# The opening rows of a fused matmul and layer norm: the last quarter of A turned by the DMA, sums put aside twice, late casts on another engine

## The chip, the cores and the metric

The kernel runs on one core of a Trainium2 chip. The metric is the time of one execution on the device in microseconds (us), the median of several runs. A profile is one further execution, recorded by the hardware: it lists every instruction of every engine with its start and its length, what it waited for, and every packet of the sixteen DMA engines.

The engines, as the profile names them: PE (the matrix unit; PEld is its loading of weights), DVE (vector), ACT (scalar), POOL (general) and SP, which here does nothing but issue DMA transfers. Each engine works through its own instructions strictly in the order of the program. Engines wait for each other and for transfers through semaphores.

## The reference

```python
x = np.matmul(a, b)                       # a, b: 2048 x 2048, float32
mean = np.mean(x, axis=-1, keepdims=True)
var = np.var(x, axis=-1, keepdims=True)
normalized = (x - mean) / np.sqrt(var + eps)
return (gamma * normalized + beta).astype(np.float32)
```

A row of the result needs the whole row of the product before its mean and variance are known.

## The kernel before

**Tiling.** A is cut into 16 row blocks of 128 rows ("rows" below, index i or p), the inner dimension into 16 k tiles of 128 (kt), the columns of B into 4 quarters of 512 (q, 0 to 3). One matmul takes one k tile of one row (128 x 128, turned so that k lies on the partitions) and one k tile of one quarter of B (128 x 512), and adds into one PSUM bank. There are 16 x 16 x 4 = 1024 of them, and eight banks. Operands are float16, sums float32. B as float16 (`b16`) stays in SBUF for the whole kernel.

**Two phases.** The first five rows (R = 5, the opening) are worked on together while B comes in: every k tile of B that lands is used by five rows. From row 5 on, all of B is there, and a row is done quarter by quarter, 16 matmuls each.

**The opening, before.** Quarter 3 is called MAIN, quarters 0, 1 and 2 ASIDE. The order of PE's work, written out by hand, is: quarters 0, 1, 2 for k tiles 0 to 3, each row's sum copied to SBUF by ScalarE (`put_aside`, L261 in the profile); then MAIN for all 16 k tiles, each row's sum copied out by `evacuate` (L95) with its statistics by VectorE (L96); then quarters 0, 1 and 2 for k tiles 4 to 15, where VectorE adds the bank to what was put aside (L265) and takes statistics (L266) in `add_rest`. After quarter 2 each row also gets its mean and variance (`stats`), and its normalisation is queued as two pieces in `backlog`, which later rows drain.

**How A gets turned.** For the opening, A comes in four chunks of four k tiles, in float32; VectorE casts a chunk to float16 (L186, L194), PE turns it with four transposes for each row (`turn`, L243), and ScalarE copies the result from PSUM to `at` (L245). From row 5 on, POOL issues a DMA that loads a whole row and casts it on the way (`a16`, L345), and SP issues a DMA transpose from `a16` to `at` (`turn_ahead`, L412). POOL's loads are held back by `gate`, a one-column copy (L255) that waits until the last block of B has landed.

**How B comes in.** `load_b2` moves two k tiles of one quarter (512 KB) into one of six staging buffers (tile `stb`, issued by SP, L203) and VectorE casts it to `b16` (L205). A staging buffer is free for the next load when its cast is done. SP also waits, at each issue, for the transfer that it issued eight before to have landed: DMA semaphores go round in eights. The blocks that come after MAIN's are in a list, `later`; `bring(n)` issues the next n of them, at fixed spots between the rows of PE's order, so that the casts lie in VectorE's order between the `add_rest` work of rows.

**After the last block of B** SP issues `gamma_b` and `beta_b` (1 MB each), four small rows of the same vectors, and then the DMA transposes of rows 5 and 6, which need POOL's loads.

Of the kernel before, what the change touches and what calls it, by code (L numbers as in the profile page):

```python
# [11 lines left out]
AluOp = mybir.AluOpType  # L12
# [4 lines left out]
def kernel(  # L17
# [9 lines left out]
    nc = tc.nc  # L27
# [5 lines left out]
    n_kt = K // P  # L33
    NB = 512
    n_nb = N // NB
    NH = N // 2
    KC = 4
    KW = KC * P
    n_kc = n_kt // KC
    R = 5  # L40
    ASIDE, MAIN = (0, 1, 2), 3
# [21 lines left out]
    gate = konst.tile([P, 1], FP32)  # L63
    gamma_b = konst.tile([P, N], FP32)
    beta_b = konst.tile([P, N], FP32)
    b16 = bpool.tile([P, n_kt, N], FP16)

    pair = {}
    xs = [None] * n_mt
    bnst = [None] * n_mt  # L70
    acc = {}

    def bank(name):
        return psum.tile([P, NB], FP32, tag="ps", name=name)
# [4 lines left out]
    def at(i):  # L79
        return pair[i // 2][:, i % 2]  # L80

    def mm(i, q, kt, first, last):
        if (i, q) not in acc:
            acc[i, q] = bank(f"acc{i}_{q}")
        nc.tensor.matmul(  # L85
            acc[i, q], at(i)[:, kt, :], b16[:, kt, ds(q * NB, NB)],
            start=first, stop=last,
        )

    def evacuate(i, q):  # L90
        if xs[i] is None:
            xs[i] = xpool.tile([P, N], FP32, tag="x", name=f"x{i}")
            bnst[i] = stat.tile([P, n_nb, 6], FP32, tag="bnst", name=f"bnst{i}")
        qs = ds(q * NB, NB)
        nc.scalar.copy(xs[i][:, qs], acc[i, q])  # L95
        nc.vector.bn_stats(bnst[i][:, q, :], xs[i][:, qs])  # L96
# [3 lines left out]
    def stats(i):  # L100
        mv = stat.tile([P, 2], FP32, tag="mv", name=f"mv{i}")
        nc.vector.bn_aggr(mv, bnst[i])  # L102
        ve = stat.tile([P, 1], FP32, tag="ve", name=f"ve{i}")
        nc.vector.tensor_tensor(ve, mv[:, 1:2], eps_t, AluOp.add)  # L104
        sq = stat.tile([P, 1], FP32, tag="sq", name=f"sq{i}")
        nc.scalar.activation(sq, ve, ActFn.Sqrt)  # L106
        return mv, sq

    def centre(i, q, mv):
        qs = ds(q * NB, NB)  # L110
        nc.vector.scalar_tensor_tensor(  # L111
            xs[i][:, qs], xs[i][:, qs], mv[:, 0:1], gamma_b[:, qs],
            AluOp.subtract, AluOp.mult)

    def scale(i, q, rstd):
        qs = ds(q * NB, NB)
        nc.vector.scalar_tensor_tensor(  # L117
            xs[i][:, qs], xs[i][:, qs], rstd, beta_b[:, qs],
            AluOp.mult, AluOp.add)

    def store(i, q0, nq):
        s = ds(q0 * NB, nq * NB)
        nc.sync.dma_start(out[ts(i, P), s], xs[i][:, s])

    def inv(i, sq):
        rstd = stat.tile([P, 1], FP32, tag="rstd", name=f"rstd{i}")
        nc.vector.reciprocal(rstd, sq)
        return rstd

    def queue_norm(i, mv, sq):  # L130

        got = {}

        def piece(q0):
            def run():
                centre(i, q0, mv)
                centre(i, q0 + 1, mv)
                if q0 == 0:
                    got["rstd"] = inv(i, sq)
                scale(i, q0, got["rstd"])  # L140
                scale(i, q0 + 1, got["rstd"])
                store(i, q0, 2)
            return run

        backlog.extend(piece(q) for q in range(0, n_nb, 2))
# [20 lines left out]
    a16_of = {}  # L166
# [15 lines left out]
    def load_a1(i, c):  # L182
        st = half_stage()
        nc.sync.dma_start(st, a[ts(i, P), ts(c, KW)])  # L184
        a16_room(i, c)
        nc.vector.tensor_copy(a16_of[i, c], st)  # L186

    def load_a2(i, c):
        st = stg.tile([P, 2, NB], FP32, tag="st", name=f"sta{i}_{c}")
        nc.sync.dma_start(  # L190
            st, a[ds(i * P, 2 * P), ts(c, KW)].rearrange("(t p) k -> p t k", p=P))
        for m in (0, 1):
            a16_room(i + m, c)
        nc.vector.tensor_copy(held["a"][:, ds(i % KC, 2), :], st)  # L194
# [3 lines left out]
        nc.sync.dma_start(st, b[ts(k, P), 0:NB])  # L198
        nc.vector.tensor_copy(b16[:, k, 0:NB], st)  # L199

    def load_b2(k, q):
        st = stg.tile([P, 2, NB], FP32, tag="st", name=f"stb{q}_{k}")
        nc.sync.dma_start(  # L203
            st, b[ds(k * P, 2 * P), ds(q * NB, NB)].rearrange("(t p) n -> p t n", p=P))
        nc.vector.tensor_copy(b16[:, k:k + 2, ds(q * NB, NB)], st)  # L205
        return st

    pairs = [list(range(i, min(i + 2, R))) for i in range(0, R, 2)]

    def load_pair(j, c):  # L210
        if len(pairs[j]) == 2:
            load_a2(pairs[j][0], c)
        else:
            load_a1(pairs[j][0], c)
# [4 lines left out]
        load_b2(0, q)  # L219
        load_b2(2, q)  # L220
    load_pair(0, 1)
    for c in range(n_kc):
        load_b2(c * KC, MAIN)
        if c + 1 < n_kc:
            load_pair(0 if c > 0 else 1, c + 1)
        load_b2(c * KC + 2, MAIN)
        if c + 1 < n_kc:
            if c > 0:
                load_pair(1, c + 1)
            load_pair(2, c + 1)  # L230

    warm = bank("warm")

# [4 lines left out]
    def turn(rows, c):  # L238
        n = len(rows)
        t_ps = psum.tile([P, n, KC, P], FP16, tag="ps", name=f"tps{rows[0]}_{c}")  # L240
        for m, i in enumerate(rows):
            for j in range(KC):
                nc.tensor.transpose(t_ps[:, m, j, :], a16_of[i, c][:, ts(j, P)], ident)  # L243
        i0 = rows[0]
        nc.scalar.copy(  # L245
            pair[i0 // 2][:, ds(i0 % 2, n), ds(c * KC, KC), :], t_ps)

    later = [(k, q) for q in ASIDE for k in range(0 if q == MAIN else KC, n_kt, 2)]

    def bring(n):  # L250
        for _ in range(n):
            k, q = later.pop(0)
            st = load_b2(k, q)
            if not later:
                nc.gpsimd.tensor_copy(gate, st[:, 0, 0:1])  # L255

    def put_aside(p, q):
        if xs[p] is None:
            xs[p] = xpool.tile([P, N], FP32, tag="x", name=f"x{p}")
            bnst[p] = stat.tile([P, n_nb, 6], FP32, tag="bnst", name=f"bnst{p}")  # L260
        nc.scalar.copy(xs[p][:, ds(q * NB, NB)], acc.pop((p, q)))  # L261

    def add_rest(p, q):
        qs = ds(q * NB, NB)
        nc.vector.tensor_tensor(xs[p][:, qs], acc[p, q], xs[p][:, qs], AluOp.add)  # L265
        nc.vector.bn_stats(bnst[p][:, q, :], xs[p][:, qs])  # L266
# [23 lines left out]
    for q in ASIDE[1:]:  # L290
# [3 lines left out]
        for p in range(R):  # L294
            for kt in range(2, KC):
                mm(p, q, kt, False, kt == KC - 1)
            put_aside(p, q)


    spots = {(0, 4): 0, (1, 1): 1, (1, 4): 2}  # L300
    for h in (0, 1):
# [3 lines left out]
            if (h, p) in spots:  # L305
                turn(pairs[spots[h, p]], 1)
    spots = {(1, 4): 0, (2, 4): 1, (3, 1): 2}
    for kt in range(KC, n_kt - KC):
        for p in range(R):
            mm(p, MAIN, kt, False, False)  # L310
            if (kt % KC, p) in spots:
                turn(pairs[spots[kt % KC, p]], kt // KC + 1)
    for kt in range(n_kt - KC, n_kt - 2):
        for p in range(R):
            mm(p, MAIN, kt, False, False)
    for p, n in enumerate((1, 1, 0, 1, 0)):
        for kt in (n_kt - 2, n_kt - 1):
            mm(p, MAIN, kt, False, kt == n_kt - 1)
        bring(n)
        evacuate(p, MAIN)  # L320


    for q, k_row, ahead, asked in (
            (0, n_kt - KC, 7, (0, 0, 1, 0, 1)), (1, 2 * KC, 2, (0, 1, 1, 1, 1))):
        bring(ahead)
        for kt in range(KC, k_row):
            for p in range(R):
                mm(p, q, kt, kt == KC, False)
        for p in range(R):
            for kt in range(k_row, n_kt):  # L330
                mm(p, q, kt, False, kt == n_kt - 1)
            bring(asked[p])
            add_rest(p, q)
    assert not later
    nc.sync.dma_start(gamma_b, gamma.unsqueeze(0).to_broadcast([P, N]))
    nc.sync.dma_start(beta_b, beta.unsqueeze(0).to_broadcast([P, N]))
    if eps_ap is not None:
# [61 lines left out]
    def quarter(i, q):  # L399
        for kt in range(n_kt):  # L400
            mm(i, q, kt, kt == 0, kt == n_kt - 1)
# [6 lines left out]
    def turn_ahead(t):  # L408
        if R <= t < n_mt:
            if t % 2 == 0:  # L410
                new_pair(t // 2)
            nc.sync.dma_start_transpose(at(t), a16[t])  # L412

    turn_ahead(R)
    turn_ahead(R + 1)
    for p in range(R):
        for kt in range(KC, n_kt):
            mm(p, ASIDE[2], kt, kt == KC, kt == n_kt - 1)
        add_rest(p, ASIDE[2])
        queue_norm(p, *stats(p))  # L420
    for i in range(R, n_mt):
        last = i == n_mt - 1
        turn_ahead(i + 2)
        for q in range(n_nb):
            quarter(i, q)
            if last and q == n_nb - 1:
                break
            evacuate(i, q)
            if q < n_nb - 1:
                drain(1)  # L430
            if last:
                scaled(i, q)
        if last:
            drain(len(backlog))
            finish_row(i)
        else:
            close(i)
# [35 lines left out]
```

## Time and profile before

| what | value |
|---|---|
| time, median of 3 runs | 246.57 us (246.26 to 246.64) |
| the profiled execution's own time | 246.04 us |
| span of its instructions | 244.0 us |
| PE busy | 236.1 us, 97% of the span |
| DVE busy | 175.3 us, 72% |
| ACT busy | 52.0 us, 21% |
| granted PE clock, mean over the span | 0.994 |
| moved by DMA | 52.64 MB, 216 GB/s on the mean |

The span is the time from the first to the last recorded instruction; the 2.0 us between it and the execution's time lie around it. The page also cuts the span into 40 slices of 6.1 us: PE is busy in tenths of 9 in all but the first and the last, and DMA in tenths of 9 in slices 2 to 17, that is up to about 100 us, with the rate near 385 GB/s up to about 50 us and falling behind it. A group line names the source line, the engine, the operation and the tiles, then busy time, mean length of one, and the idle time of the engine just before these instructions with what ended it. A timeline line gives start and length in us, and in brackets the idle time before it and who ended that.

### The profile page before, as it was taken

Reading aid. Unit: us, or ns where it says so; the run is one execution under the profiler, and the core shown is the slowest. Engines: PE = TensorE matmul, PEld = TensorE weight load, DVE = VectorE, ACT = ScalarE, POOL = GpSimd, SP = SyncE. Lnnn points to the kernel's source line nnn. Section 1 sums busy time; section 2 is a strip of 40 time slices with the busy share of each in tenths; the row PEclk is TensorE's granted clock in tenths of the full one; section 3 lists DMA queues with packets and bytes.
Section 4 is the critical chain, followed back from the end, with each engine's and each line's share of the span. In section 5 each row is a group of like instructions: output and inputs, shape, how many; then the busy total and the mean of one; then the engine's idle time right before and its main releaser. Section 6 shows DMA issues by size and latency. Waiting matters only on the chain.

```text
span 244.0 us, 2967 instructions
## 1 busy us (share of the span) xinstructions
PE 236.1 (97%) x1133; PEld 107.7 (44%) x1133; DVE 175.3 (72%) x310; ACT 52.0 (21%) x96; POOL 7.0 (3%) x17
## 2 busy tenths in 40 slices
PE   7899999999999999999999999999999999999982
PEld 2344555444444444444444444444444444444430
DVE  1544554969997589999999995937557391947873
ACT  2466445400000011212120211112111211112100
POOL 0000000000300100000000000000000000000000
PEclk9999999999999999999999999999999999999997
DMA  5999999999999999898989898683907144220405
GB/s 118 395 387 387 387 381 385 379 309 364 375 261 179 159 131 262 245 230 216 232 220 272 134 291 174 202 194 64 257 4 197 60 128 132 82 90 0 176 0 172
DMA packets 41190, 52.64 MB, mean 216 GB/s; under 512 B 24404, under 2 KB 24404, under 8 KB 40920
## 3 DMA queue, kind: packets, MB, share of 16 engines
q1 hardware_dynamic: 39592, 46.68, 60.1%
q0 software_dynamic: 1584, 5.77, 15.2%
q8 instruction: 9, 0.15, 0.3%
q14 instruction: 5, 0.04, 0.1%
HBM read 35.67 MB, written 16.78 MB: 215 GB/s over the span
## 4 chain that ended last, share of the span: by engine, by line
PE 94%; DMA 2%; DVE 1%; SPq 0%; issue 0%; ACT 0%
PE acc L85 91%; DMA st<-in_a_dram 2%; PE tps L243 2%; PE w L385 1%; DVE x L395 0%; DVE bnst L369 0%; DVE x L372 0%; DVE a16s L186 0%; PE warm L236 0%; SPq L198 0%; SPq L184 0%; PE nm_ps L380 0%; DVE mv L102 0%; ACT lead L381 0%; DVE nm L377 0%
## 5 line engine op out<-in xcount | busy, mean ns | idle before, releaser
L85 PE MATMUL acc<-b,at 128*128 128x512 f16 x1024 | 223.2, 379 | 0.9 <-DVE b L199 0.9
L85 PEld LDWEIGHTS <-at 128*128 128x128 f16 x1024 | 99.6, 98 | 119.3 <-ACT at L245 1.4
L96 DVE BATCH_NORM_STATS2 bnst<-x 128x6 f32<-128x512 f32 x48 | 32.9, 689 | 33.4 <-ACT x L95 33.3
L95 ACT COPY x<-acc 128x512 f32<-128x512 f32 x48 | 27.8, 588 | 108.8 <-PE acc L85 107.5
L117 DVE SCALAR_TENSOR_TENSOR x<-x,rstd,beta_b 128x512 f32<-128x512 f32 x61 | 43.1, 747 | 0.5
L111 DVE SCALAR_TENSOR_TENSOR x<-x,mv,gamma_b 128x512 f32<-128x512 f32 x60 | 42.0, 742 | 0.0
L205 DVE CAST b<-stb 128x1024 f16<-128x1024 f32 x30 | 20.4, 688 | 11.2 <-DMA stb<-in_b_dram 11.1
L106 ACT ACTIVATE sq<-ve 128x1 f32<-128x1 f32 x16 | 3.2, 203 | 55.3 <-DVE ve L104 55.3
L245 ACT COPY at<-tps 128x512 f16<-128x512 f16 (+1 forms) x14 | 10.6, 770 | 14.1 <-PE tps L243 13.8
L265 DVE TENSOR_TENSOR x<-acc,x 128x512 f32<-128x512 f32 x15 | 10.3, 686 | 3.0 <-PE acc L85 2.9
L266 DVE BATCH_NORM_STATS2 bnst<-x 128x6 f32<-128x512 f32 x15 | 10.4, 694 | 0.5
L345 POOL DMA_DIRECT2D a<-in_a_dram x11 | 6.3, 576 | 91.7 <-DMA at<-a 91.3
L236 PE MATMUL warm<-zeros 128*128 128x512 f16 x23 | 7.7, 478 | 1.2 <-DVE zeros L152 1.2
L261 ACT COPY x<-acc 128x512 f32<-128x512 f32 x15 | 7.6, 607 | 5.1 <-PE acc L85 5.1
L186 DVE CAST a16s<-st 128x512 f16<-128x512 f32 x8 | 3.4, 427 | 6.1 <-DMA st<-in_a_dram 5.9
L243 PEld LDWEIGHTS <-a16s 128*128 128x128 f16 x80 | 5.2, 98 | 4.4 <-DVE a16s L186 2.3
L194 DVE CAST a16s<-sta 128x1024 f16<-128x1024 f32 x6 | 4.2, 695 | 4.1 <-DMA sta<-in_a_dram 4.1
L243 PE MATMUL tps<-ident,a16s 128*128 128x128 f16 x80 | 6.8, 220 | 0.2
L236 PEld LDWEIGHTS <-zeros 128*128 128x128 f16 x23 | 2.5, 115 | 4.9 <-issue 2.7
L102 DVE BATCH_NORM_AGGREGATE mv<-bnst 128x2 f32<-128x24 f32 x16 | 4.2, 264 | 0.5
L199 DVE CAST b<-st 128x512 f16<-128x512 f32 x4 | 1.7, 427 | 2.3 <-DMA st<-in_b_dram 2.3
L104 DVE TENSOR_TENSOR ve<-mv,eps_t 128x1 f32<-128x1 f32 x16 | 2.5, 159 | 0.5
(26 smaller groups left out, 16.8 us busy)
## 6 DMA issues: line engine op xcount, KB each, us to landing
stb<-in_b_dram SPq DMA_DIRECT2D x30, 512.0 KB, 6.5
out_dram<-x SPq DMA_DIRECT2D x30, 512.0 KB, 3.0
a<-in_a_dram POOLq DMA_DIRECT2D x11, 512.0 KB, 7.2
sta<-in_a_dram SPq DMA_DIRECT2D x6, 512.0 KB, 6.4
st<-in_a_dram SPq DMA_DIRECT2D x8, 256.0 KB, 7.2
st<-in_b_dram SPq DMA_DIRECT2D x4, 256.0 KB, 6.3
gamma_b<-in_gamma_dram SPq DMA_DIRECT2D x1, 1024.0 KB, 6.8
beta_b<-in_beta_dram SPq DMA_DIRECT2D x1, 1024.0 KB, 10.3
```

The costliest lines, as they stand in the source:

```text
L85: nc.tensor.matmul(acc[i, q], at(i)[:, kt, :], b16[:, kt, ds(q * NB, NB)], start=first, stop=last,)
L95: nc.scalar.copy(xs[i][:, qs], acc[i, q])
L96: nc.vector.bn_stats(bnst[i][:, q, :], xs[i][:, qs])
L111: nc.vector.scalar_tensor_tensor(xs[i][:, qs], xs[i][:, qs], mv[:, 0:1], gamma_b[:, qs], AluOp.subtract, AluOp.mult)
L117: nc.vector.scalar_tensor_tensor(xs[i][:, qs], xs[i][:, qs], rstd, beta_b[:, qs], AluOp.mult, AluOp.add)
L205: nc.vector.tensor_copy(b16[:, k:k + 2, ds(q * NB, NB)], st)
L236: nc.tensor.matmul(warm if to is None else to, zeros[:, 0:P], zeros, start=True, stop=True)
L243: nc.tensor.transpose(t_ps[:, m, j, :], a16_of[i, c][:, ts(j, P)], ident)
L245: nc.scalar.copy(pair[i0 // 2][:, ds(i0 % 2, n), ds(c * KC, KC), :], t_ps)
L261: nc.scalar.copy(xs[p][:, ds(q * NB, NB)], acc.pop((p, q)))
L265: nc.vector.tensor_tensor(xs[p][:, qs], acc[p, q], xs[p][:, qs], AluOp.add)
L266: nc.vector.bn_stats(bnst[p][:, q, :], xs[p][:, qs])
```

## The change

The opening is put in another order, and three pieces of work go to other places.

- Chunk 3 of A (k tiles 12 to 15 of the five rows) is still loaded and cast as before, but PE no longer turns it. SP issues one DMA transpose of 128 x 512 for each row instead (`turn_last`, five in all), between the issues of late blocks of B.
- MAIN stops after k tile 11 and is put aside; quarter 0 continues with k tiles 4 to 11 and is added to what was put aside (`add_part`, the same vector addition as L265 without statistics). Quarters 1 and 2 run from 4 to 15 as before, with the last four k tiles row by row. Then MAIN and quarter 0 get k tiles 12 to 15, row by row, with `add_rest`; the last one also closes the row (`close_opening`).
- The loads are reordered accordingly: MAIN's and quarter 0's blocks 12 and 14 move to the end of the list; chunk 3 of A comes after MAIN's and part of quarter 0's blocks. Everything of `later` (14 blocks) is issued in one go, with no regard to PE's order, and cast by ScalarE instead of VectorE.

```diff
-    def load_b2(k, q):
+    def load_b2(k, q, cast=nc.vector.tensor_copy):
...
-        nc.vector.tensor_copy(b16[:, k:k + 2, ds(q * NB, NB)], st)
+        cast(b16[:, k:k + 2, ds(q * NB, NB)], st)
...
-    for c in range(n_kc):
+    K3 = n_kt - KC
+    for c in range(n_kc - 1):
         load_b2(c * KC, MAIN)
-        if c + 1 < n_kc:
+        if c + 2 < n_kc:
             load_pair(0 if c > 0 else 1, c + 1)
         load_b2(c * KC + 2, MAIN)
-        if c + 1 < n_kc:
+        if c + 2 < n_kc:
             if c > 0:
                 load_pair(1, c + 1)
             load_pair(2, c + 1)
+    load_b2(KC, 0)
+    load_b2(KC + 2, 0)
+    for j in range(len(pairs)):
+        load_pair(j, n_kc - 1)
+        if j < 2:
+            load_b2(2 * KC + 2 * j, 0)
+    load_b2(KC, 1)
+    load_b2(KC + 2, 1)
...
+    def turn_last(i):
+        nc.sync.dma_start_transpose(at(i)[:, ds(K3, KC), :], a16_of[i, n_kc - 1])
...
+    def add_part(p, q):
+        qs = ds(q * NB, NB)
+        nc.vector.tensor_tensor(xs[p][:, qs], acc.pop((p, q)), xs[p][:, qs], AluOp.add)
...
+    def part(q, k0, k1, k_row, done):
+        for kt in range(k0, k_row):
+            for p in range(R):
+                mm(p, q, kt, kt == k0, False)
+        for p in range(R):
+            for kt in range(k_row, k1):
+                mm(p, q, kt, kt == k0, kt == k1 - 1)
+            done(p, q)
...
-    for kt in range(KC, n_kt - KC):
+    for kt in range(KC, K3 - 2):
         for p in range(R):
             mm(p, MAIN, kt, False, False)
-            if (kt % KC, p) in spots:
+            if kt < 2 * KC and (kt % KC, p) in spots:
                 turn(pairs[spots[kt % KC, p]], kt // KC + 1)
...
+    for p in range(R):
+        for kt in (K3 - 2, K3 - 1):
+            mm(p, MAIN, kt, False, kt == K3 - 1)
+        put_aside(p, MAIN)
+
+    later = [(k, 1) for k in range(2 * KC, n_kt, 2)]
+    later += [(k, 2) for k in range(KC, n_kt, 2)]
+    later += [(k, q) for q in (MAIN, 0) for k in range(K3, n_kt, 2)]
+    for n, (k, q) in enumerate(later):
+        for i in range(2 * n, min(2 * n + 2, R)):
+            turn_last(i)
+        st = load_b2(k, q, nc.scalar.copy)
+    nc.gpsimd.tensor_copy(gate, st[:, 0, 0:1])
+
+    part(0, KC, K3, K3 - 2, add_part)
+    part(1, KC, n_kt, K3, add_rest)
+    part(2, KC, n_kt, K3, add_rest)
...
-    for p in range(R):
-        for kt in range(KC, n_kt):
-            mm(p, ASIDE[2], kt, kt == KC, kt == n_kt - 1)
-        add_rest(p, ASIDE[2])
+    def close_opening(p, q):
+        add_rest(p, q)
         queue_norm(p, *stats(p))
+
+    part(MAIN, K3, n_kt, K3, add_rest)
+    part(0, K3, n_kt, K3, close_opening)
```

More of the change, by code (lines that the diff above doesn't have):

```diff
@@ L246, in turn @@
             pair[i0 // 2][:, ds(i0 % 2, n), ds(c * KC, KC), :], t_ps)
[L248 to L255, printed above, removed]
+    def turn_last(i):
+        nc.sync.dma_start_transpose(at(i)[:, ds(K3, KC), :], a16_of[i, n_kc - 1])
     def put_aside(p, q):
@@ L307 @@
     spots = {(1, 4): 0, (2, 4): 1, (3, 1): 2}
-    for kt in range(KC, n_kt - KC):
+    for kt in range(KC, K3 - 2):
         for p in range(R):
             mm(p, MAIN, kt, False, False)
-            if (kt % KC, p) in spots:
+            if kt < 2 * KC and (kt % KC, p) in spots:
                 turn(pairs[spots[kt % KC, p]], kt // KC + 1)
-    for kt in range(n_kt - KC, n_kt - 2):
-        for p in range(R):
[L315 to L334, printed above, removed]
+    for p in range(R):
[13 more added lines that the diff above has]
+    part(2, KC, n_kt, K3, add_rest)
     nc.sync.dma_start(gamma_b, gamma.unsqueeze(0).to_broadcast([P, N]))
@@ L415 @@
     turn_ahead(R + 1)
-    for p in range(R):
-        for kt in range(KC, n_kt):
-            mm(p, ASIDE[2], kt, kt == KC, kt == n_kt - 1)
-        add_rest(p, ASIDE[2])
+    def close_opening(p, q):
+        add_rest(p, q)
         queue_norm(p, *stats(p))
+    part(MAIN, K3, n_kt, K3, add_rest)
+    part(0, K3, n_kt, K3, close_opening)
     for i in range(R, n_mt):
```

## The prediction

> **What bounds the kernel now.** I read the page's busy times, the chain that ended last (totals, then its pieces in order of time), and, since every change lies before row 5, the timelines of DVE, POOL and SP up to 90 us, with busy time by stretch for the DMA.
>
> ```profile
> PE 236.1 (97%) x1133; PEld 107.7 (44%) x1133; DVE 175.3 (72%) x310; ACT 52.0 (21%) x96; POOL 7.0 (3%) x17
> ...
> 35.94 0.45 PE tps L243 x8
> 36.38 1.08 PE acc L85 x5
> 37.46 0.45 PE tps L243 x8
> 37.91 0.43 PE acc L85 x2
> 38.34 0.22 PE tps L243 x4
> 38.56 195.77 PE acc L85 x907
> ```
>
> PE is the chain: 907 matmuls in 195.77 us are 0.216 us each, without a hole. The three tps pieces are the turning of chunk 3: 20 transposes. Row 5's first matmul starts at 82.2 us (in the trace; 704 matmuls before the chain's PE part ends at 234.33, by 0.216, give the same within 0.2). A saving in the opening counts only if what row 5 needs is there earlier too. Who brings that:
>
> ```profile
> 64.48 0.18 POOL L255 COPY gate<-stb 128x1 f32<-128x1 f32 x1 [62.91 <-DMA stb<-in_b_dram]
> 65.03 2.10 POOL L345 DMA_DIRECT2D a<-in_a_dram  x3 [0.37 <-issue]
> 80.65 0.53 POOL L345 DMA_DIRECT2D a<-in_a_dram  x1 [13.52 <-DMA at<-a]
> ...
> 73.27 12.97 SPq L412 DMA_TRANSPOSE at<-a  x3
> ```
>
> The last block of B lands at 64.4; the gate opens; row 5 of A is loaded by 73.25 and turned by 80.1 (its landing, which POOL's wait in the third line follows). So 15.7 us lie between B's last landing and row 5's operand, and the slack to PE is 82.2 - 80.1 = 2.1 us. Nothing on the chain shows this, because nobody waits yet.
>
> The DMA that sets 64.4:
>
> ```profile
> 14.00:38.00 24.00, 24.00 (x155) 12.50 (x153) 11.97 (x19) 13.27 (x23) 0.00 (x0) 1.00 1.05 384
> ...
> 48.00:56.00 8.00, 8.00 (x39) 3.60 (x37) 5.88 (x10) 0.00 (x0) 0.00 (x0) 1.00 0.94 304
> ...
> 75.50:82.20 6.70, 6.70 (x32) 3.04 (x31) 4.61 (x11) 0.61 (x3) 0.53 (x1) 1.00 1.18 174
> ...
> 158.50:161.10 2.60, 2.60 (x14) 1.17 (x13) 1.49 (x3) 0.47 (x1) 0.00 (x0) 1.00 1.16 225
> ...
> 31.68 0.69 DVE L205 CAST b<-stb 128x1024 f16<-128x1024 f32 x1 [0.83 <-DMA stb<-in_b_dram]
> ...
> 40.44 0.69 DVE L205 CAST b<-stb 128x1024 f16<-128x1024 f32 x1 [0.66 <-DMA stb<-in_b_dram]
> ```
>
> The last two columns are DMA share and GB/s. Loading runs at a share of 1.05, that is, full; only 48 to 56 is thin (0.94). The two casts wait for landings and stand 6.5 blocks of 512 KB apart: 1.35 us a block. The other two stretches are DMA transposes of whole rows: two back to back with a rest of other loads (6.7 us), and one alone (2.6 us).
>
> **The change part by part.**
>
> *PE loses 20 transposes:* 0.45 + 0.45 + 0.22 = 1.12 us, all on the chain. The matmuls stay 1024. PE would reach row 5 at 82.2 - 1.1 = 81.1. Three ACT copies (2.6 us) go too, off the path.
>
> *Five DMA transposes of 128 KB come into the full load queue.* A whole row has four times the size. Bounds for one: 2.6/4 = 0.65 us from the one alone; 6.7/8 = 0.84 from the pair; and 2.4 from the third (83.4 to 93.2, interleaved with POOL's loads on another queue). Below: its packets at the fastest stretch of the pair (1130 per us of 256 bytes) give 0.45. Here no other queue is active, but the five come in three groups and each must follow on loads. I take 0.75, between the first two rows: 3.75 us together, ends 2.25 and 12. All of it delays later blocks, since the queue is full.
>
> *The new place of the last block.* MAIN's block 8 keeps its place (cast at 31.68). Then come nine and a half blocks up to quarter 1's block 6: 31.7 + 12.8 = 44.5. Then 14 late blocks, 18.9: 63.4. (In the old order the same bytes took to 64.4, as VectorE's order held staging buffers in the thin stretch.) With the transposes 63.4 + 3.75 = 67.2. The gate, POOL's loads and gamma and beta follow in the same order as before, so row 5's operand is there at 67.2 + 15.7 = 82.8, against 81.1 on PE: a stall of 1.7 us.
>
> *SP's queue.* A transpose's issue took 1.9 to 6.1 us for a row (L412), so 0.5 to 1.5 here; 14 loads queue behind. SP spends 0.37 on a load and has 1.35, and by its waits it issues about 6 us ahead of landing (the load issued at 33.84 landed at 40.4). The first transpose needs chunk 3's cast (37.8), which is over when SP gets there; the last needs that of row 4 (about 42.4). Five of 0.8 are 4 us of SP spread over 6 us: covered by the 6 us of queued transfers. At 1.5 each the cover is used up and 1 to 2 us are lost: kept for the range. The transposes also take five turns in the round of eight semaphores; eight outstanding are still about 7 us of work. I cost it at nothing.
>
> *Late casts on ScalarE.* 14 casts; the nearest row is its copy of as many elements, L245, 1.01 us; twice the 512-wide copy is 1.18. Both below the 1.35 between landings, and ScalarE has nothing else after MAIN's `put_aside` (before, its five copies took 2.54 us). Zero, at most 0.5 us on each block's readiness against VectorE's 0.69.
>
> *Are the blocks there for PE?* Without transposes and stalls, MAIN ends at about 38.1, quarter 0 at 46.7, quarter 1 at 59.7, quarter 2 at 72.6. MAIN's block 10 lands 1.3 earlier than before; quarter 0's block 4 is cast by 35.1 for 38.1. Tightest is quarter 1's block 14: it lands at 44.5 + 3.75 + 4 x 1.35 = 53.7, cast by 54.8, needed at 55.8. From 0.95 us for a transpose it would be late, but a stall here only replaces part of the one at row 5. Blocks 12 and 14 of MAIN and quarter 0 have 9 us or more.
>
> *VectorE.* 14 casts go (9.6 us), ten additions of 0.69 come (6.9). The place matters: fifteen sums now end 0.86 us apart, from 69.1 on (quarter 2, MAIN, quarter 0), while addition and statistics take 1.3, and the last five 1.9 with the mean. VectorE falls behind by some 10 us, done at about 92. PE waits only for banks: eight sums later the bank is used again, and the addition that frees it ends 5 us ahead of the ninth sum and 2 us ahead of the sixteenth, row 5's first (69.1 + 7 x 1.33 + 0.7 = 79.1 against 81.2). No stall. The rows behind inherit a lag of about 6 us, when VectorE is full until about 150 us; row 7 needs row 0's buffer at 112, and its store, issued at 93.30 before, would land by about 104. Covered.
>
> *Sum:* -1.1 + 1.7 = +0.6 us. The profiled execution's 246.04 becomes 246.6; it stood 0.5 below the median, so 247.2.
>
> [...] Row: a transpose of 512 KB takes 2.6 us alone, a load of 512 KB 1.35. [...]
>
> **The rivals.**
>
> 1. *Transposes are hidden (faster).* If the five together cost under 2 us, the operand is there at 81.1 and the whole 1.1 us is won: 245.5. It turns at 0.40 us for one; at 0.62 nothing is won or lost. For it: packets at 0.45 in the best stretch, and the slack of the chain behind the gate, which may come out a microsecond shorter, as row 5's turning took 6.9 us and later ones 5.0. Against: no whole row went below 0.65 for a quarter.
>
> 2. *Transposes crawl, or starve the load queue.* The third one took 9.8 us at 159 GB/s, and its issue held SP for 6 us. At 1.3 us or more for a piece, or with SP's cover gone: row 5 at 85.5 or later, a stall of 4.5: +3.4, 250. Against: that one shared the engines with another queue; here loads and transposes are in one.
>
> 3. *VectorE's lag is the bound.* If the late rows' stores held `xs` buffers back. For it: DVE is in tenths of 9 from about 90 to 150. Against: PE can run seven quarters of 3.45 us ahead on eight banks. It would take a lag of over 15 us; perhaps +1: 247.5 without other stalls.
>
> **How the numbers follow.** A stall at row 5 between 1 and 3.5 us: chance 0.57, 246.5 to 249, likeliest 247.2. Hidden or nearly: 0.25, 245.4 to 246. Crawling: 0.13. VectorE: 0.05. The range reaches from the full gain, 245.4, to halfway into the crawling case, 249.6; it leaves out about one in ten. About 0.2% (0.5 us) is what a measurement of this kernel can tell from no change. Faster: the hidden case, 0.25. The likeliest case is within 0.5 us of 246.57 when a piece costs 0.52 to 0.72, some 0.18; slower is the rest, 0.57.
>
> **What would show it.** L243 has 60 transposes, not 80. POOL's gate stands near 67 instead of 64.5, the first DMA transposes at about 38 on SP. PE has one hole of about 1.7 us, before the first matmul of row 5, with a DMA (at<-a) as releaser, and none in quarter 1. ACT shows 14 casts of about 1 us, none late for PE. Wrong would be: a gate at or before 65.5 (the pieces are cheap or the queue was not full), holes in quarter 1 (they crawl), or holes ended by DVE.

## The result, and the profile after

The changed kernel takes 246.95 us (median of 22 runs, 246.21 to 249.13); the kernel before, on the same chip, 246.33 us (22 runs, 245.77 to 247.54). The ratio is 1.0037, with a 95% interval of 1.0023 to 1.0051: slower by 0.9 us (0.6 to 1.3). The profiled execution took 246.69 us against 246.04.

Where it went is on the chain that ended last. These are its pieces up to row 5 (start, length, what):

```profile
67.97 0.18 POOL gate L344
...
68.53 7.32 DMA a<-in_a_dram
75.85 0.02 issue
75.86 7.30 DMA at<-a
83.16 0.05 issue
83.21 152.13 PE acc L85 x704
```

Before, the chain was PE alone from the first chunk of A on. Now everything ahead of row 5 is the gate, the load of row 5 and its transpose; PE comes in at 83.21 for the last 704 matmuls. The timeline of PE, cut off at 110 us, has the hole itself:

```profile
33.13 48.29 PE L85 MATMUL acc<-b,at 128*128 128x512 f16 x223
83.21 27.15 PE L85 MATMUL acc<-b,at 128*128 128x512 f16 x125 [1.78 <-DMA at<-a]
```

223 matmuls follow each other without a gap, so every late block of B and every turned chunk was there in time. Then 1.78 us are lost to a transpose. The saving is there too, in the page's busy times and costliest groups:

```profile
PE 235.3 (96%) x1113; PEld 106.6 (44%) x1113; DVE 172.5 (71%) x306; ACT 62.9 (26%) x107; POOL 6.6 (3%) x17
...
L205 ACT CAST b<-stb 128x1024 f16<-128x1024 f32 x14 | 14.6, 1045 | 15.2 <-DMA stb<-in_b_dram 15.2
...
L252 PE MATMUL tps<-ident,a16s 128*128 128x128 f16 x60 | 5.3, 223 | 0.5 <-DVE a16s L186 0.4
```

60 transposes on PE instead of 80. ScalarE's casts take 1.045 us each and wait only for landings.

What pushed the gate back is in the stretches of the DMA while the five new transposes pass (the last two columns are DMA share and GB/s; a share over 1 means that the recorded times of packets overlap, as at 1.05 while loading, or reach past the end of the stretch):

```profile
42.00:42.50 0.50, 0.50 (x4) 0.26 (x3) 0.15 (x1) 0.00 (x0) 0.00 (x0) 1.00 1.04 406
42.50:43.50 1.00, 1.00 (x7) 0.41 (x6) 0.28 (x1) 0.00 (x0) 0.00 (x0) 1.00 2.38 333
43.50:45.00 1.50, 1.50 (x8) 0.68 (x7) 0.69 (x1) 0.00 (x0) 0.00 (x0) 1.00 0.98 65
45.00:45.50 0.50, 0.50 (x4) 0.26 (x3) 0.17 (x1) 0.00 (x0) 0.00 (x0) 1.00 1.41 289
...
47.00:48.00 1.00, 1.00 (x6) 0.44 (x5) 1.00 (x3) 0.32 (x1) 0.00 (x0) 1.00 1.28 294
...
49.30:49.90 0.60, 0.60 (x4) 0.29 (x3) 0.00 (x0) 0.00 (x0) 0.00 (x0) 1.00 1.50 287
```

The transposes' packets (256 bytes each) come in three clusters: the first two transposes from 42.55 to 45.55, the next two from 46.99 to 47.95, the last one from 49.35 to 49.87. The first cluster takes 3.0 us, of which 1.5 pass at 65 GB/s with the engines counted as busy. In the records the last 25 packets of earlier loads end there, from 43.9 on one after the other, the last at 44.45; and 18 of the cluster's 1024 transposing packets last over 0.5 us, up to 1.99, where the usual one lasts 18 ns. The second cluster takes 0.96 us for as many bytes and has no such packet. So the price is not by the piece: the first group to meet the load queue pays more than the others, which take some 0.5 us a piece. The records do not name the engine of a packet, so what held these packets is not shown.

### The profile page after: what moved, and what is told of

The parts are those of the page before. It is cut to its first block, busy times and chain, and to the rows that moved or that the text cites. A ratio compares the mean times of both kernels' runs of the same rounds, so it can differ in the third digit from the quotient of the medians.

```text
span 244.6 us, 2953 instructions
## 1 busy us (share of the span) xinstructions
PE 235.3 (96%) x1113; PEld 106.6 (44%) x1113; DVE 172.5 (71%) x306; ACT 62.9 (26%) x107; POOL 6.6 (3%) x17
## 4 chain that ended last, share of the span: by engine, by line
PE 63%; issue 28%; DMA 6%; DVE 1%; POOL 0%; ACT 0%; POOLq 0%
PE acc L85 62%; DMA a<-in_a_dram 3%; DMA at<-a 3%; PE w L400 1%; DVE x L410 0%; DVE bnst L384 0%; DVE x L387 0%; PE nm_ps L395 0%; POOL ident L154 0%; DVE mv L102 0%; DVE zeros L152 0%; ACT lead L396 0%; POOL gate L344 0%; DVE nm L392 0%; DVE ve L104 0%
## 5 line engine op out<-in xcount | busy, mean ns | idle before, releaser
L95 ACT COPY x<-acc 128x512 f32<-128x512 f32 x43 | 24.6, 584 | 78.2 <-PE acc L85 78.2
L272 DVE TENSOR_TENSOR x<-acc,x 128x512 f32<-128x512 f32 x20 | 13.5, 674 | 13.7 <-PE acc L85 13.7
L205 DVE CAST b<-stb 128x1024 f16<-128x1024 f32 x16 | 11.1, 694 | 11.3 <-DMA stb<-in_b_dram 11.3
L205 ACT CAST b<-stb 128x1024 f16<-128x1024 f32 x14 | 14.6, 1045 | 15.2 <-DMA stb<-in_b_dram 15.2
L264 ACT COPY x<-acc 128x512 f32<-128x512 f32 x20 | 10.2, 607 | 7.5 <-PE acc L85 7.5
L254 ACT COPY at<-tps 128x512 f16<-128x512 f16 (+1 forms) x11 | 8.0, 741 | 11.4 <-PE tps L252 11.1
L252 PE MATMUL tps<-ident,a16s 128*128 128x128 f16 x60 | 5.3, 223 | 0.5 <-DVE a16s L186 0.4
L252 PEld LDWEIGHTS <-a16s 128*128 128x128 f16 x60 | 4.0, 100 | 4.0 <-DVE a16s L186 2.6
```

The lines of the kernel that those rows point to most:

```text
L205: cast(b16[:, k:k + 2, ds(q * NB, NB)], st)
L254: nc.scalar.copy(pair[i0 // 2][:, ds(i0 % 2, n), ds(c * KC, KC), :], t_ps)
```

## The experiments

The theory: *row 5's operand is the whole loss*; it hangs on the gate, the gate on the last block of B, and that block on the transposes ahead of it in the queue. The rivals: the new order of the opening or ScalarE's casts cost something themselves, or VectorE's lag does; and, on the price, the transposes cost by the piece or by the first meeting. Ratios are to runs of the kernel before on the same chip in the same session: 246.11 us (35 runs) for e1 to e4, 245.83 (17 runs) for e5, e6, e7 and e9, and one run of 246.38 for e10 and e11. The changed kernel was timed in yet another session, and stands beside these by its own ratio, 1.0037. Clock times of gates and operands are from one profile of each kernel.

### Chunk 3 turned by PE again, all else as changed

```diff
+    def turn_pe(rows):        # four PE transposes a row, VectorE copies PSUM to at
+        ...
     for n, (k, q) in enumerate(later):
-        for i in range(2 * n, min(2 * n + 2, R)):
-            turn_last(i)
         st = load_b2(k, q, nc.scalar.copy)
-    part(1, KC, n_kt, K3, add_rest)
+    part(1, KC, n_kt, K3, add_rest, {(KC + 1, 1): 0, (KC + 2, 1): 1, (KC + 3, 1): 2})
```

> The changed kernel with chunk 3 of A turned by PE again (20 transposes between the matmuls of quarter 1, VectorE copying the result), the new order, ScalarE's casts and everything else kept. Theory 'queue' (the five DMA transposes lengthen the full load queue, the last block of B lands later, row 5's operand with it): the gate opens at 63.4 to 64.4 us instead of 68.0, the operand is there by 79.5, PE needs it at 82.5, so there is no hole; the 1.1 us of transposes are back: 246.3, as before the change, 0.6 below the changed kernel. Rival 'order' (the late gate comes from the new order of loads or from staging buffers freed later by ScalarE): the gate stays near 68, the operand at 83.2 meets a PE that is ready at 82.5, a hole of 0.7: 247.0, as changed.

Measured: 245.82 us, ratio 0.998 (0.9965 to 0.9995). The timelines of POOL, and of PE (cut off at 110 us):

```profile
63.58 0.18 POOL L354 COPY gate<-stb 128x1 f32<-128x1 f32 x1 [62.01 <-DMA stb<-in_b_dram]
```
```profile
51.54 58.65 PE L85 MATMUL acc<-b,at 128*128 128x512 f16 x271
```

Without the DMA transposes the gate opens at 63.58, row 5's operand is there at 77.72, and PE has no hole. The five transposes therefore cost 67.97 - 63.58 = 4.4 us of the load queue. The order, the late casts and VectorE's ten additions are all still in this kernel, and it is not slower than the one before: they cost nothing that can be measured. That it is 0.2% faster, with as many transposes on PE as before, was not explained by any run.

### Two of the five rows by DMA, and one

```diff
     for n, (k, q) in enumerate(later):
-        for i in range(2 * n, min(2 * n + 2, R)):
+        for i in range(2 * n, min(2 * n + 2, 2)):   # e9: ..., 1)
             turn_last(i)
+    # the other rows by turn_pe in quarter 1, as in the experiment above
```

> The changed kernel with two DMA transposes (rows 0 and 1) instead of five; rows 2, 3 and 4 of chunk 3 are turned by PE (12 transposes, 0.67 us). Theory 'queue', with the 0.7 to 0.9 us for each that the changed kernel's gate implies: the gate at 65 to 66, the operand at 80.5 to 81.2, PE ready at 82.1: no hole, and 0.45 us of PE saved against before: 245.9. If the price is not by the piece but by the first group that meets the loads: the gate at 66.5 or later, the operand at 81.8, hardly a hole, 246.0. Rival 'order': gate near 68, a hole of 1.1, 247.0.

> The changed kernel with one DMA transpose (row 0), the other four rows of chunk 3 turned by PE (0.9 us). Two measured runs stand: five transposes put the gate at 67.8 to 68.0, two at 67.1, none at 63.6. If the price is by the piece (0.75 as predicted, or 0.9 as five of them would make it): gate at 64.4 to 64.6. If the first transpose that meets the loads pays by itself (all engines wait until the last one has caught up, some 2.5 us) and each piece only 0.5: gate at 66.3 to 66.8.

Measured: with two 245.92 us, ratio 0.999 (0.9968 to 1.0012); with one 245.37 us, a single run. The gate of each, with two first:

```profile
67.06 0.18 POOL L356 COPY gate<-stb 128x1 f32<-128x1 f32 x1 [65.49 <-DMA stb<-in_b_dram]
```
```profile
65.49 0.18 POOL L356 COPY gate<-stb 128x1 f32<-128x1 f32 x1 [63.92 <-DMA stb<-in_b_dram]
```

Against 63.58 with none and 67.97 with five: the first piece costs 1.9 us, the first two 3.5, and the three after them 0.9 together. By the piece (4.4/5) one would have moved the gate to 64.5 and two to 65.3; the gate stands 1.0 and 1.7 us later. One alone stays below what the first meeting was expected to cost if it were a fixed price, so it is neither a price by the piece nor one flat fee.

The gates also carry what differed between the profiles before any transpose had sent a packet: e2's loads ran 1.0 us behind e1's at that point, e6's 0.6 us ahead. This can be taken out. Both kernels load the same packets of 2 KB; the lag of the n-th of them to land behind e1's n-th, read just before and just behind a group, is the price of the group alone. One piece then costs 1.8 us (e9) and two 2.8 (e2). In the profiles with the same five pieces (the changed kernel, e3, e4, e6) the first two cost 2.2 to 2.4, the next two 1.0 and the last one 0.8: 4.0 to 4.2 together, though the last packet of B ends 3.0 to 4.4 us later than in e1. The first group is the dear one by this count too, and a first group of two costs less than twice a first one. With two the row 5 operand came at 81.87, and PE did not wait there, having turned three rows itself.

### Gamma and beta behind the transposes of rows 5 and 6

```diff
-    nc.sync.dma_start(gamma_b, gamma.unsqueeze(0).to_broadcast([P, N]))
-    nc.sync.dma_start(beta_b, beta.unsqueeze(0).to_broadcast([P, N]))
...
     turn_ahead(R + 1)
+    nc.sync.dma_start(gamma_b, gamma.unsqueeze(0).to_broadcast([P, N]))
+    nc.sync.dma_start(beta_b, beta.unsqueeze(0).to_broadcast([P, N]))
```

> The changed kernel with the two 1 MB loads of gamma and beta issued behind the DMA transposes of rows 5 and 6 instead of ahead of them; they are needed from about 93 us on. The five DMA transposes stay. Theory 'queue': the gate stays at 68.0, but row 5's load no longer waits behind 5 us of gamma and beta: it starts 1 to 1.5 us earlier, the operand at 81.5 to 82.3 against 81.4, a hole of 0.1 to 0.9 instead of 1.8: 245.2 to 246.0. Rival 'elsewhere' (the loss is VectorE's lag behind row 5, the hole is only where it shows): the time stays at 246.9.

Measured: 245.46 us (244.43 to 246.62), ratio 0.9968 (0.9947 to 0.9989). PE's timeline, cut off at 110 us:

```profile
33.15 77.22 PE L85 MATMUL acc<-b,at 128*128 128x512 f16 x357
```

The hole is gone although the gate, at 67.81, stands where it stood: POOL's load sends its first packet at 69.73 instead of 70.96, has the engines to itself (SP issues nothing from 65.4 to 73.46), and the operand is there at 81.05, some 0.4 us ahead of PE. That is the profiled execution, of 244.67 us. Four of the twelve runs lie at 244.4 to 244.7 and eight at 245.3 to 246.6; with so little slack the slower ones may still have a hole, which no profile here shows. The five transposes are still in the queue, at the same price. What is lost in the changed kernel is thus not their time but row 5's.

The control, the same edit in the kernel before:

> The kernel before, with the loads of gamma and beta issued behind the DMA transposes of rows 5 and 6, as in the run with the changed kernel. Theory 'queue': row 5's operand comes 1.5 to 3 us earlier, about 77.5 to 78.5, against a PE that is ready at 82.2 either way: the profile shows no hole before or after and the same span, 244.0. In the timed runs the slack of 2.1 us grows to about 4; if the operand's arrival varies by more than that from run to run, the slower runs go and the median falls by 0.2 to 0.4: 245.8; if it doesn't, 246.1. Rival 'elsewhere' (the late gamma helps by itself, for example by freeing the engines for other loads): the same 0.3% gain as in the changed kernel against the changed one, which was 1.5 us: 244.8.

Measured: 245.79 us, ratio 0.9994 (0.9985 to 1.0003), operand at 77.95 and no hole. Where PE does not wait, an earlier operand buys nothing: the gain above is the changed kernel's hole, and not something that gamma's place gives to any kernel.

### The gate two blocks earlier

```diff
         st = load_b2(k, q, nc.scalar.copy)
-    nc.gpsimd.tensor_copy(gate, st[:, 0, 0:1])
+        if n == len(later) - 3:
+            nc.gpsimd.tensor_copy(gate, st[:, 0, 0:1])
```

> The changed kernel with the gate on the twelfth of the fourteen late blocks instead of the last, so that POOL's loads of rows 5 to 7 may start two blocks earlier; nothing else moved. Theory 'queue': the gate opens at 65.3 instead of 68.0. If POOL's loads share the engines with SP's queue, the operand is there at 80.5 to 81.5, the hole is gone or nearly, 245.1 to 245.4. If they get the engines only when SP's queue is through with gamma and beta, as the traces before and after suggest (first packet at 68.1 and 71.0, when those end), the operand stays near 83 and the time at 246.9. Rival 'elsewhere': 246.9 whatever the gate does.

Measured: 246.64 us, ratio 1.0023 (0.9999 to 1.0047). POOL's and PE's timelines:

```profile
64.88 0.18 POOL L345 COPY gate<-stb 128x1 f32<-128x1 f32 x1 [63.31 <-DMA stb<-in_b_dram]
```
```profile
82.49 27.80 PE L85 MATMUL acc<-b,at 128*128 128x512 f16 x128 [1.17 <-DMA at<-a]
```

The gate opens 3.1 us earlier and the operand is there only 0.7 us earlier (82.44). POOL issues the load at 65.44, and its first packet is seen at 69.27, 3.8 us on, while gamma and beta fill the other queue. It does not wait until they are through, as the expectation's second case had it: their last packets end at 74.5, and the two run side by side from 69.3 on. Opening the gate is not the same as getting the engines.

### Both edits together

> The changed kernel with both: the gate on the twelfth late block, and gamma and beta behind the transposes of rows 5 and 6. With the gate alone POOL's first packet stayed at 69.3, when SP's queue ran dry. Here that queue is dry after the last block of B, near 67. Theory 'queue', with POOL's loads served only then: first packet at 66.5 to 67.5, two to three us earlier than with gamma late alone (69.7), the operand at 78.5 to 79.5 against 81.4: no hole and 2 us of slack; the whole saving of PE stays, 245.0 to 245.3, and the runs spread less than in the run with gamma late alone. If the queues share the engines, first packet at 65.7 and the blocks of B a little later, which have 9 us: the same time. Rival 'elsewhere': no better than gamma late alone, 245.5.

Measured: 244.40 us (244.12 to 245.08), ratio 0.9937 (0.9923 to 0.9952). The gate and the load in POOL's timeline, and PE's (cut off at 110 us):

```profile
63.78 0.18 POOL L345 COPY gate<-stb 128x1 f32<-128x1 f32 x1 [62.21 <-DMA stb<-in_b_dram]
64.33 1.73 POOL L359 DMA_DIRECT2D a<-in_a_dram  x3 [0.37 <-issue]
```
```profile
32.59 77.65 PE L85 MATMUL acc<-b,at 128*128 128x512 f16 x359
```

The load's first packet follows its issue by 1.4 us (65.71), the operand is there at 78.22, 5 us earlier than in the changed kernel, and PE runs through. Of the 5 us, 1.4 are not the edit's: in this profile the last packet of B ends at 66.0 instead of 67.4, and the loads were 1.1 us ahead already before the first transpose's packet. The first packet at 65.7 is what the expectation gave for queues that share the engines; but it overlaps B's last packets by only 0.3 us, so this run hardly tells that case from a load that is served when SP's queue is dry. The six runs lie within 1.0 us, against 2.2 for the edit of gamma and beta alone, which fits a slack of 2.7 us. This version beats both kernels: the change's saving is real, and it was row 5's operand that withheld it. The gain, 1.4 us (1.2 to 1.9 by the interval), is a little more than the 1.12 us of transposes saved; PE's long stretch also began at 32.59 instead of 33.13 in its profile, and the runs leave open why.

### The late casts on VectorE again

```diff
-        st = load_b2(k, q, nc.scalar.copy)
+        st = load_b2(k, q)
```

> The changed kernel with the 14 late casts on VectorE again, in the place where the program has them (ahead of quarter 0's additions in VectorE's order). It prices the cover that the casts on ScalarE give. The last cast ends at about 68.5; only then the additions of quarter 0 free their banks. PE has three banks to spare and stops early in quarter 1, at about 47.5, for some 20 us: 265 to 270, with DVE as what ends the hole. If the casts on ScalarE were only a convenience: 247.

Measured: 270.12 us, a single run. PE's timeline, cut off at 110 us:

```profile
69.99 40.19 PE L85 MATMUL acc<-b,at 128*128 128x512 f16 x173 [22.89 <-DVE x L268]
```

The 14 blocks are asked for in one go, so with VectorE as the caster all 14 casts stand in its order ahead of quarter 0's additions. Those free the PSUM banks; PE fills the banks and stands still for 22.9 us until the last block has landed and VectorE gets to L268. The move to ScalarE costs nothing, as e1 shows, and asking for the blocks in one go, with the casts at this place, cannot do without it.

### A sixth transpose, early in the queue

Is it the meeting of loads and transposes that costs, and does one meeting spare the next? A spare transpose of 128 KB into the place of `gamma_b`, which is written again later, was added at two spots:

```diff
             load_pair(2, c + 1)
+        if c == 1:      # e10
+            nc.sync.dma_start_transpose(gamma_b[...], a16_of[0, 1])
...
     for j in range(len(pairs)):
+        if j == 2:      # e11
+            nc.sync.dma_start_transpose(gamma_b[...], a16_of[0, 2])
         load_pair(j, n_kc - 1)
```

> The changed kernel with one more DMA transpose of 128 KB, into a place that is overwritten later, issued at about 24 us among the opening's loads, to land near 31. So far the first group of transposes held the engines for 2.4 to 3.8 us, whether one, two or, with three following, five pieces, and the later groups took 0.5 us a piece. If the engines are out of step from the start and one transpose brings them into step for good: the extra one costs 2 to 3 us, the group near 43 to 46 then only 1.0 (0.5 a piece), and the gate stays near 68.0 to 68.5. If they fall out of step anew, by drift or by a single event: the group near 45 takes 2.5 to 4 again and the gate comes at 70 to 71. In both cases the blocks of MAIN land later by the extra piece, and PE may stall a microsecond near 30.

> The same with the extra transpose issued at about 35 us, to land near 41, four blocks ahead of the first group. Event between 41 and 45 (an instruction fetch of 16 KB occupied one engine for 1.04 us at 43.2 in the changed kernel's profile): the extra one is cheap or dear by itself, and the group still takes 2.5 us or more; gate at 70 or later if both are dear, 68.5 if only the group is. Slow drift over tens of microseconds: the extra one takes 2.5 to 3.5, the group right behind it only 1.0 to 1.3; gate at 68.0 to 68.7.

Measured: 253.78 and 252.46 us, a single run each. In e10 the spare one's packets lie at 27.43 to 30.39, in e11 at 38.43 to 41.35: 2.9 to 3.0 us each, for one piece; by the lag of the loads behind e1's they cost 2.4 and 1.6. The five behind were not spared: by the same count their first group cost 2.5 and 2.6. The slow stretches of the spare piece and of the first group behind it, in e10 and then in e11:

```profile
28.40:30.30 1.90, 1.90 (x12) 0.76 (x10) 1.22 (x2) 0.59 (x1) 0.00 (x0) 1.00 0.62 51
...
45.00:46.20 1.20, 1.20 (x7) 0.57 (x6) 0.00 (x0) 0.00 (x0) 0.00 (x0) 1.00 2.31 40
```
```profile
39.40:41.30 1.90, 1.90 (x11) 0.84 (x10) 0.69 (x1) 0.00 (x0) 0.00 (x0) 1.00 1.18 153
...
45.10:46.50 1.40, 1.40 (x8) 0.65 (x7) 0.35 (x1) 0.00 (x0) 0.00 (x0) 1.00 2.06 42
```

Here, too, 1.2 to 1.9 us pass at 51, 40, 153 and 42 GB/s, where a loading stretch has 385. In e11 only 3.3 us lie between the end of the spare piece and the first of the five, and the group pays again, 2.7 us. *Why* a first group is so dear stays open. A suspect was one engine held by an instruction fetch of 16 KB (1.04 us, at 43.2 in the changed kernel's records): one lay near the dear group there, but none was near the spare piece of e10 or of e11. So the fetch is not needed for it; whether it adds to it was not settled.

These two kernels show something else. PE already stands still in quarter 1, for 0.9 us in e10 and 2.5 us in e11, behind VectorE's additions and, in e11, a late block. The gates come at 70.82 and 71.23, and PE's holes at row 5 grow to 3.80 and 2.90 us. In the timelines of PE, e10 and then e11:

```profile
86.67 154.85 PE L85 MATMUL acc<-b,at 128*128 128x512 f16 x704 [3.80 <-DMA at<-a]
```
```profile
86.78 153.81 PE L85 MATMUL acc<-b,at 128*128 128x512 f16 x704 [2.90 <-DVE bnst L275]
```

In e11 the line names VectorE's statistics, which end at 86.74. The load of weights ahead of that matmul, which reads row 5's operand, waits as long for the transpose:

```profile
86.77 0.55 PEld L85 LDWEIGHTS <-at 128*128 128x128 f16 x4 [3.39 <-DMA at<-a]
```

So the operand alone would have kept PE waiting until then. The same 704 matmuls took 152.13 us in the changed kernel; here they took 2.7 and 1.7 us more. The stretches of e11 behind its hole say why (the third column from the end is the granted clock):

```profile
86.70:87.30 0.60, 0.52 (x3) 0.29 (x4) 0.53 (x4) 0.05 (x1) 0.04 (x1) 1.00 1.17 216
87.30:90.70 3.40, 3.40 (x10) 1.20 (x9) 3.20 (x7) 0.36 (x2) 1.02 (x2) 0.50 0.87 132
90.70:92.00 1.30, 1.30 (x8) 0.56 (x6) 1.26 (x3) 0.20 (x1) 0.00 (x0) 0.99 1.11 197
```

For 3.4 us after a hole of 2.9 the granted clock is 0.50; 3.4 us at half speed are 1.7 us lost, which is the 1.7 above. In e10 it is 0.50 for 6.8 us, from 85.4 to 92.2, of which PE works 5.6; half of that is 2.8, and 2.7 us are lost. The hole of 1.78 us in the changed kernel left the clock at 1.00.

## Why the prediction was right, point by point

The forecast was 247.2 with a stall at row 5 as the likeliest case; the median is 246.95, and the stall is there, in its place, with the predicted releaser. Against the kernel before, the forecast was +0.6 us: the profiled executions differ by 0.65, the medians of the session by 0.6, the ratio says 0.9. The forecast for the profile, 246.6, met 246.69; to get from it to the median, it added the 0.5 us by which three runs stood above the profile before, and over 22 runs that is 0.3.

- **PE loses 20 transposes, 1.12 us, PE ready at 81.1.** Ready at 81.42. The start of its long stretch varies by up to 0.6 us between the profiles of these kernels (32.59 to 33.16).
- **The last block without the transposes at 63.4.** e1's gate is at 63.58: right within 0.2.
- **Five transposes at 0.75 each, 3.75 us, gate at 67.2.** 4.4 us by the gates, gate at 67.97; 4.0 to 4.2 by the lag of the loads. The sum is off by 0.3 to 0.65 and the way to it was wrong: the term was worked out by the piece from whole rows' transposes, and the cost is that of the first group (2.2 to 2.4) with 1.0 and 0.8 for the two groups behind it. That the two ways meet near 4 is luck of five pieces in three groups; for one piece alone (e9) the forecast's 0.75 would have been short by 1.0 to 1.15.
- **From the gate to the operand 15.7 us.** 15.2 (67.95 to 83.16), 0.5 shorter. The load, from issue to landing, took 7.3 us instead of 8.2, as its first packet came 2.4 us after the issue instead of 3.1; the turning took 7.3 instead of 6.9.
- **A stall of 1.7 us.** 1.78. The errors of these steps, 0.8 late at the gate, 0.5 early behind it, 0.3 late on PE, nearly cancel; the stall is right partly for that reason.
- **SP costed at nothing, 0.5 to 1.5 us an issue.** The result holds, the size does not: in SP's timeline, x2, x2 and x1 are groups of transposes, with start and length ahead of them:

```profile
38.18 3.16 SPq L258 DMA_TRANSPOSE at<-a16s  x2
...
42.06 3.30 SPq L258 DMA_TRANSPOSE at<-a16s  x2
...
46.08 1.20 SPq L258 DMA_TRANSPOSE at<-a16s  x1
```

  7.7 us for five, 1.5 each, the upper end; the prediction feared 1 to 2 us lost from there on. The load queue ran thin only for moments: the DMA share is 0.88 and 0.93 from 39 to 41, 0.80 from 49.9 to 50.5 and 0.92 from 52.5 to 53.5, against 1.05 when full. By these shares that is worth some 0.5 us, an estimate. That the dear first group gave SP some 2 us more of cover is likely, but no run shows it.
- **ScalarE's casts at nothing, 1.01 to 1.18 us, quarter 1's block 14 cast by 54.8.** 1.045 us; that block's cast ran from 53.79 to 54.83. PE's 223 matmuls in a row show that nothing was late.
- **VectorE behind by some 10 us, done at about 92, no stall.** Its last work for the five rows ends at 92.06, and no idle time of PE between 33 us and the last matmul was ended by it. e1 carries the same additions and loses nothing.

Rival 1, the transposes hidden, needed all five under 2 us; they cost 4.4, and even the cheap ones, 0.5 a piece, stand above the 0.34 that a load of as many bytes takes, a quarter of the 1.35 us of a block. Rival 2, the crawl, needed 1.3 us a piece: the first group comes near it (1.1 to 1.2 a piece by the lag of the loads) and the others do not; the spare transposes of e10 and e11, at 2.4 and 1.6 us for one piece, show how near it is, and with a sixth piece and the clock's fall behind it these kernels end where rival 2 had put it and beyond. Rival 3, VectorE, did not show in the changed kernel.

What the prediction did not have is that a hole can cost more than its length (in e11 2.90 us and 1.7 more, in e10 3.80 and 2.7 more). The changed kernel's runs spread further upwards (to 249.13) than those of before (to 247.54), and the slowest has a granted clock of 0.983 on the mean, against 0.994 in the profiled one. A hole that is a microsecond longer there, with the clock's fall behind it, would fit. The next three (249.12, 248.61 and 248.24) do not bear it out: their clocks, 0.989, 0.988 and 0.996, are no lower than those of runs at 246.8 and 246.4 (0.989, 0.988). No profile shows such an execution, so what makes these runs long stays open.

## What to carry to other kernels

Work that moves from the bounding engine to a full transfer queue pushes back everything that queues behind it (here the gate, by 4.4 us): follow the chain that hangs on the last transfer (here the gate, a load, a transpose) to the next phase, and compare its slack, 2.1 us here, with what is put in front. If the slack is spent, first take out of that chain what need not be in it; moving gamma and beta back and opening the gate earlier turned 0.9 us lost into 1.4 us won, and neither was enough of itself to gain that. Do not price a transposing DMA among loads by its bytes: here the first group that met the loads cost some 2 to 3 us and the later ones 0.5 to 0.8 a piece. Whether all five in one group would be cheaper still, no run here shows.

## What the runs showed of the hardware

- A DMA transpose of 128 KB that met a running load queue held the loads back by 1.8 (e9), 2.4 (e10) and 1.6 us (e11), two of them together by 2.2 to 2.8 us (e2, and the first group of the kernels with five); further ones a few loads later cost 0.5 to 0.8 us each in those kernels. In e11 a first piece did not spare a group 3.3 us behind it.
- A load issued by POOL sent its first packet 1.4 us after its issue when SP's queue was empty (e3, e5) or down to the last packets of B (e6), and 2.4 to 3.8 us after it when that queue was full of broadcasts (the changed kernel and e4).
- The granted clock of PE stayed at 1.00 after a hole of 1.8 us (the changed kernel). It was 0.50 for 3.4 us, from 87.3 on, after one of 2.9 (e11), for 6.8 us, from 85.4 on, with one of 3.8 (e10), and in e7 from 51.4 on, through the 22.9 us hole and 5.3 us beyond it. From the start of the hole to the fall these are 3.4, 2.5 and 4.3 us, so no fixed delay shows; in e11 PE had worked again for half a microsecond when the clock fell. No run here has a hole between 1.8 and 2.9 us, so where it turns stays open.
